# Zero products around two routing stages and a layer boundary of a two-layer trunk, and a new fence for the splits of weights

## The chip, the cores and the metric

The kernel runs on one core of a Trainium2 chip, as one launch. The metric is device time in microseconds; a run's time is that of its slowest core, and here there is only one. Three runs of the kernel before took 848.1, 848.4 and 856.6 us; the median is 848.4 us.

## The reference, cut to what matters

Two layers work on 256 tokens of width 1024. Each layer has two halves:

```
h  = rms_norm(x, g) * (1 + sc1) + sh1          # sc, sh, g come from the condition c
z  = h @ w_in                                  # 1024 x 2840
y  = concat(retention, gmlp, sparse attention) @ w_out
x  = x + g1 * y
h2 = rms_norm(x, g') * (1 + sc2) + sh2
x  = x + g2 * grouped_moe(h2)                  # 16 experts, best group, top 2 in it
```

In `rms_norm` each token is multiplied by `rsqrt(mean(x*x) + eps)`. The router of the mixture needs the logits of all 16 experts, a softmax, the best group of four and the best two experts in it. Only then is it known which tokens go to which expert.

## The kernel before, in words

**Layout.** The residual `xT` lies in SBUF as 128 partitions by 8 chunks by 256 tokens, so a chunk `c` is a block of 128 channels. Everything is float32, and the products that must be exact are made from two float32r parts: an operand is split into a high part `hi` and a low part `lo = x - hi`, and `mm3` makes three products (hi hi, hi lo, lo hi).

**Weights.** They are read from HBM once, in 1 MB pieces, by SyncE's queue into a ring of 11 slots (`slot`, `slots`). A slot is free again when the last product that reads it is done, so the queue runs ahead of TensorE by what the ring holds.

**A layer.** `rms_r` (L312) makes the mean of squares: for each chunk ScalarE squares `xT[:, c, :]` (L316), and TensorE multiplies the square by a constant matrix `onesd` (L317). These eight products, called mean products here, add up in one PSUM bank `pm`. ScalarE then takes a logarithm (L321) and an exponential (L322) of it, which gives `r`. For each chunk VectorE makes `ht` (L420), ScalarE makes the high part `hhi` (L421) and VectorE the low part `hlo` (L422). Then come the input projections `dz` and `tm` (products at L350 to L352, written to `pz`). Each weight block of 128 x 512 is first split by `whl` (L338): ScalarE copies the high part (L344), and VectorE, or GpSimd for one block in three in this layer, subtracts to get the low part (L346). Five buffers hold split blocks. After the mixers come the output projection (`pw`) and the routing stage, called the seam here.

**The seam.** In `moe` VectorE goes through a chain of some thirty small instructions from the logits (`lg`, L873) to the chosen experts (`o1`, L924). TensorE ranks the tokens of each expert with five small products (`prank`, L936 to L940), VectorE makes one-hot tables `Pm` (L1227), TensorE gathers the tokens with them (L980), and the first expert's products (`pgu`, L1051) can begin. The four PSUM banks `mo` that collect the experts' outputs are opened by products of a zero block with zeros (L948), 128 x 512 in bfloat16. `WARM` says how many rounds of four there are: one in the first layer, six in the second.

**The mixture.** Sixteen experts are worked through in four groups: `up` (L1051) or `up_few` (L1060), an activation, a transposition, `down`, and `combine` or `combine_few`, whose products add to `mo`. At the end eight VectorE instructions add `mo` to `xT` (L1310).

**The boundary between the layers.** The mixture of the first layer returns a list `fence`: a product, the last ScalarE instruction that evicts an expert's output, and the last addition to `xT`. In the second layer every split in `whl` is ordered behind the second of these on ScalarE and the third on VectorE, by `tc.issue_after`, which only orders instructions of the same engine.

**What sets the order.** A planner orders each engine's instructions before the kernel runs. It takes them by the order of the program, but an instruction that is not ready by its own estimate of time is passed over for a later one that is. So the zero products at L948 stand after `prank` in the program and run before it. The order is then fixed: each engine works through its instructions in it.

Of the kernel before, what the change touches and what calls it, by code (L numbers as in the profile page):

```python
# [17 lines left out]
S = 256  # L18
# [20 lines left out]
NOVF = 8  # L39
OVE = 12  # L40
OFL = True
WARM = (1, 6)
WV = (0, 1, 5)
NPA = ("0011", "0011")
S4P = ("01111111", "01111111")
# [30 lines left out]
def trunk(tc, I, out):  # L76
    nc = tc.nc
    P = 128
    V, A, G, T, Y = nc.vector, nc.scalar, nc.gpsimd, nc.tensor, nc.sync
# [3 lines left out]
    with ctx:  # L83
# [7 lines left out]
        def tl(cls, shape, name, dt=F32):  # L91
            return up.tile([P] + shape, dt, tag=cls, name=name, bufs=NB[cls])
# [4 lines left out]
        def bank(tag="W", name="pw"):  # L97
            return ps.tile([P, 512], F32, tag=tag if ND else "b", name=name, bufs=(ND if tag == "D" else 8 - ND))
# [24 lines left out]
        onesd = cp.tile([P, P], F32, name="onesd")  # L123
# [15 lines left out]
        def exp_ln_tables():  # L139
            return A.preload_act_table_set("natural_log_exp_and_others")  # L140
# [122 lines left out]
        zb = cp.tile([P, P], BF16, name="zb")  # L263
# [44 lines left out]
        def tables(after):  # L308
            with tc.issue_after(after):
                exp_ln_tables()  # L310

        def rms_r(l, src, last=None):  # L312
            pm = bank("W", "pm")
            for c in range(8):
                sq = tl("k1", [S], "sq")
                sq_ = A.activation(sq, src[:, c, :], AF.Square)  # L316
                T.matmul(pm[:, :S], onesd, sq, start=c == 0, stop=c == 7)  # L317
            if last is not None:
                last(sq_.ins)
            r = tl("k1", [S], "r")  # L320
            A.activation(r, pm[:, :S], AF.Ln, bias=epsc[:, 0:1])  # L321
            A.activation(r, r, AF.Exp, scale=-0.5)  # L322
            return r

        def rms(l, gname, vs, vc, src):
            gs = sml([8], "gs", bufs=2)
            V.scalar_tensor_tensor(gs, mod(l, vc), 1.0, smv(l, gname), op0=OP.add, op1=OP.mult)
            r = rms_r(l, src)
            h = tl("b8", [8, S], "h")
            for c in range(8):  # L330
                t = tl("k1", [S], "ht")
                V.scalar_tensor_tensor(t, src[:, c, :], gs[:, c:c + 1], r, op0=OP.mult, op1=OP.mult)
                A.activation(h[:, c, :], t, AF.Identity, bias=mod(l, vs)[:, c:c + 1])
            return h
# [3 lines left out]
        def whl(wv, n):  # L338
            hl = tl("wh", [2, 512], "whl", F32R)
            hi, lo = hl[:, 0, :n], hl[:, 1, :n]  # L340
            with contextlib.ExitStack() as st:
                for i_ in fence[1:]:
                    st.enter_context(tc.issue_after(i_))
                A.copy(hi, wv)  # L344
                wc[0] += 1
                (G if wc[0] % WP[fl[0]] == 0 else V).tensor_tensor(lo, wv, hi.bitcast(F32), op=OP.subtract)  # L346
            return hi, lo
# [25 lines left out]
        fence = []  # L373
        for l in range(L):
# [30 lines left out]
            if True:  # L405
                pp = up
                r = rms_r(l, xT, angles if l == 0 else tables)
                hhi = tl("b8", [8, S], "hhi", F32R)
                hlo = tl("b8", [8, S], "hlo", F32R)
# [41 lines left out]
                def dz(idx, dst_fn, tag="D"):  # L451
                    pz = [bank(tag, "pz") for _ in range(2)]

                    def step(c):
                        w = whl(ld[f"s{idx}"][c // 4][:, 512 * (c % 4):512 * (c % 4) + 512], 512)
                        for t in range(4):
                            d = slice(P * t, P * t + P)
                            mm3(pz[t // 2][:, S * (t % 2):S * (t % 2) + S], (w[0][:, d], w[1][:, d]),
                                (hhi[:, c, :], hlo[:, c, :]), c == 0 and t % 2 == 0, c == 7)
                        if c == 7:  # L460
                            for t in range(2):
                                dst_fn(2 * t, pz[t].rearrange("p (u n) -> p u n", u=2))
                    return step

                def tm(idx, n, dst_fn, tag="D"):
                    pz = [bank(tag, "pz") for _ in range(2)]

                    def step(c):
                        w = whl(ld[f"s{idx}"][c // 4][:, n * (c % 4):n * (c % 4) + n], n)
                        for tt in range(2):  # L470
                            d = slice(P * tt, P * tt + P)
                            mm3(pz[tt][:, :n], (hhi[:, c, d], hlo[:, c, d]), w, c == 0, c == 7)
                        if c == 7:
                            for tt in range(2):
                                dst_fn(tt, pz[tt])
                    return step
# [42 lines left out]
                for kv in range(2):  # L519
                    pd = bank("W", "pd")  # L520
                    for g in range(2):
                        for hh in range(2):
                            T.matmul(pd[64 * hh:64 * hh + 64, S * g:S * g + S], ident[:, 64 * g:64 * g + 64], zkc[:, kv, :],
                                     start=True, stop=True, skip_group_check=True)
# [237 lines left out]
                for t in range(2):  # L762
                    pg = bank("W", "pg")
                    for n in range(2):
                        for hh in range(2):
                            g = 2 * t + hh
                            T.matmul(pg[64 * hh:64 * hh + 64, P * n:P * n + P], gv[:, n, 64 * g:64 * g + 64], wsT[:, g, :],
                                     start=True, stop=True)
# [7 lines left out]
                def wsplit(k, hf):  # L776
                    return whl(ld[f"o{k // 4}"][k % 4 // 2][:, 1024 * (k % 2) + 512 * hf:1024 * (k % 2) + 512 * hf + 512], 512)
# [20 lines left out]
                for hf in range(2):  # L798
# [21 lines left out]
                    for tt in range(2):  # L820
# [3 lines left out]
                        sq = tl("t2", [512], "sqt")  # L824
# [4 lines left out]
                    for u in range(4):  # L829
                        T.matmul(pq[32 * u:32 * u + 32, :S], rwg[:, 4 * hf + u, :], xT[:, 4 * hf + u, :], start=hf == 0, stop=hf == 1,  # L830
                                 skip_group_check=True)
                lq = tl("k1", [S], "lq")
                V.tensor_copy(lq, pq[:, :S])
                for tt in range(2):
                    T.matmul(pl[:, 16 * tt:16 * tt + 16], lq[:, P * tt:P * tt + P], sel4, start=True, stop=True)
            fence[:] = moe(tc, nc, l, locals())
        for c in (0, 4, 2, 6):
            Y.dma_start(out[:, c:c + 2, :], xT[:, c:c + 2, :])


def moe(tc, nc, l, env):
    g_ = dict(env)
    I, slots, bank, rms, mod, xT = (g_[k] for k in ("I", "slots", "bank", "rms", "mod", "xT"))
    ident, rw, rb, ub, oneb, zb, iot, W4 = (g_[k] for k in ("ident", "rw", "rb", "ub", "oneb", "zb", "iot", "W4"))
    P = 128
    V, A, G, T, Y = nc.vector, nc.scalar, nc.gpsimd, nc.tensor, nc.sync
    reuse = []

    def kept(mk):
        def f(*a, **kw):  # L850
            if not reuse:
                return mk(*a, **kw)
            key = (mk, {"paT": "ppg", "pth": "ppg", "py": "pgx"}.get(a[-1], a[-1])) if mk is bank_ else (mk, a[2] if mk is tl_ else a[1])
            if key not in reuse[0]:
                reuse[0][key] = mk(*a, **kw)
            return reuse[0][key]
        return f
    tl_, sml_, bank_ = g_["tl"], g_["sml"], bank
    tl, sml, bank = kept(tl_), kept(sml_), kept(bank_)
    mp = None  # L860
    if True:
# [84 lines left out]
        mo = [bank("D", f"mo{i}") for i in range(4)]  # L946
        for i in [0, 1, 2, 3] * WARM[l]:
            T.matmul(mo[i], zb, zb.unsqueeze(1).to_broadcast([P, 4, P]), start=True, stop=False, skip_group_check=True)  # L948
# [96 lines left out]
        lastu = [None]  # L1045
# [80 lines left out]
        def combine_few(yy, pT):  # L1126
            for u in range(2):
                for i in range(2):
                    for q in range(4):
                        r_ = slice(SW * q, SW * q + SW)  # L1130
                        T.matmul(mo[q][:, S * u:S * u + S], yy[i][r_, P * u:P * u + P], pT[r_, :], start=False, stop=False,  # L1131
                                 skip_group_check=True)

        def extras():
            cu, capc = g_["cu"], g_["capc"]
# [110 lines left out]
        pm0, last = [None], [None, None, None]  # L1246
        xgs = group(0, lambda tt, p, k: rk[:, tt, ST0 + p:ST0 + p + k])
        pend, seen, done = None, -1, []
        for g4, members in enumerate(XGR):
            order = members  # L1250
            for k, (p, xo_, w) in enumerate(order):
# [23 lines left out]
                def tables_():  # L1275
                    if p == "x":
                        return scatter_tables(one_hot(rkx, w), gP, HOT)
                    if e < NST:
                        return scatter_tables(one_hot(rk[:, :, ST0 + e], w), gate, ST0 + e)
                    return scatter_tables(one_hot(rkP[:, :, e], w), gP, e)  # L1280
# [4 lines left out]
                pT, gc = tables_()  # L1285
                if pend:
                    aT = turn(pend[0])
                    yy = (down_few if pend[4] else down)(aT, *pend[1:4])
# [15 lines left out]
                if seen == RES:  # L1304
                    last[2] = lastu[0]
        done.pop(0)()
        combine_few(down_few(turn(pend[0]), *pend[1:4]), pend[2])
        for m in (0, 2, 4, 6, 1, 3, 5, 7):
            b, u = m // 2, m % 2
            last[1] = V.scalar_tensor_tensor(xT[:, m, :], mo[b][:, S * u:S * u + S], mod(l, 5)[:, m:m + 1], xT[:, m, :],  # L1310
                                   op0=OP.mult, op1=OP.add).ins
        return [last[2]] + last[:2]


def pack(inp):
# [73 lines left out]
```

## Time and profile before

| what | value |
|---|---|
| runs | 848.1, 848.4, 856.6 us, median 848.4 |
| the profiled execution | 856.05 us |
| its span, first to last instruction | 854.5 us |
| TensorE busy | 762.8 us (89%) |
| VectorE busy | 459.3 us (54%) |
| ScalarE busy | 273.4 us (32%) |
| mean granted clock of TensorE | 0.929 of full speed |
| read from HBM | 290.84 MB |

Read the table with the span in mind: 1.55 us of the profiled execution lie around it. TensorE is granted full speed (1.00, the 2.4 GHz level) or half of it (0.50, the 1.2 GHz level); a mean between them in a stretch says that the clock changed in it. A busy TensorE at half speed is doing half the work. The profiled execution is one of the longer ones: it stands 7.65 us above the median of the runs.

### The profile page before, as it was taken

What the parts mean: (1) busy time and instruction counts of PE and PEld (TensorE: products, weight loads), DVE (VectorE), ACT (ScalarE), POOL (GpSimd) and SP (SyncE); (2) the same over time, 40 slices, a digit from 0 to 9 for tenths busy, and PEclk for the clock granted to TensorE, in tenths of its full rate; (3) what the DMA queues carried; (4) which work ended last, traced back from release to release, by engine and by line L of the source; (5) the groups of instructions that cost most, each with busy time, mean ns of one, the idle gap of its engine ahead of it and who ended that gap; (6) DMA issues with size and microseconds to landing.
All of it is one profiled execution on the core that took longest, in us unless ns stands there. A gap on an engine that the chain in (4) does not pass through costs nothing. (4 is left out here: it accounts for less than half of the span.)

```text
span 854.5 us, 14344 instructions
## 1 busy us (share of the span) xinstructions
PE 762.8 (89%) x5460; PEld 480.2 (56%) x5460; DVE 459.3 (54%) x1189; ACT 273.4 (32%) x655; POOL 68.0 (8%) x83
## 2 busy tenths in 40 slices
PE   3789999976999999887988998999999999979795
PEld 2677665775535455343448886678744545534342
DVE  6997959986833223211245998598582322312123
ACT  6246555633111111110135646466311201101010
POOL 2232200120000000000003231002000000000000
PEclk9899869979899999989999996699999999998798
DMA  8959818979799999999999489178878999999993
GB/s 354 420 224 354 321 45 296 395 275 383 304 381 418 417 418 419 418 420 413 421 417 379 156 300 389 58 265 323 318 283 303 359 421 415 419 418 418 416 418 145
DMA packets 47169, 292.95 MB, mean 343 GB/s; under 512 B 5488, under 2 KB 6256, under 8 KB 16496
## 3 DMA queue, kind: packets, MB, share of 16 engines
q1 hardware_dynamic: 45648, 289.76, 85.3%
q10 hardware_dynamic: 1440, 2.16, 0.8%
q8 instruction: 46, 0.75, 0.3%
q14 instruction: 35, 0.29, 0.1%
HBM read 290.84 MB, written 1.05 MB: 342 GB/s over the span
## 5 line engine op out<-in xcount | busy, mean ns | idle before, releaser
L1051 PE MATMUL pgu<-w1slot,xg 128*64 128x512 f32 x640 | 168.5, 623 | 18.3 <-PEq L1188 9.8
L1051 PEld LDWEIGHTS pgu<-w1slot,xg 128*64 128x64 f32 x640 | 51.7, 141 | 101.0 <-issue 97.9
L193 DVE SCALAR_TENSOR_TENSOR adaslot<-adaslot,sb__90 128x1024 f32<-128x1024 f32 x72 | 94.5, 1324 | 0.0
L1093 DVE SCALAR_TENSOR_TENSOR yy<-py,gc,yy 64x512 fp32r<-64x512 f32 x40 | 30.0, 750 | 108.6 <-ACT yy L1092 108.6
L350 PE MATMUL pz<-hhi,whl 128*128 128x256 f32 x256 | 75.0, 304 | 10.2 <-ACT hhi L421 10.2
L351 PE MATMUL pz<-hlo,whl 128*128 128x256 f32 x256 | 76.1, 301 | 0.9 <-DVE hlo L422 0.7
L352 PE MATMUL pz<-hhi,whl 128*128 128x256 f32 x256 | 76.3, 304 | 0.5 <-DVE whl L346 0.4
L1092 ACT ACTIVATE yy<-py,gc 64x512 fp32r<-64x512 f32 x40 | 27.3, 683 | 151.5 <-PE py L1084 135.3
L346 POOL TENSOR_TENSOR whl<-winslot,whl 128x512 fp32r<-128x512 f32 (+1 forms) x24 | 34.2, 1425 | 370.7 <-DMA winslot<-win_dram 239.7
L1060 PE MATMUL pgu<-w1slot,xg 128*32 128x256 f32 x896 | 58.4, 382 | 5.2 <-DMA w1slot<-w_dram 5.2
L350 PEld LDWEIGHTS pz<-hhi,whl 128*128 128x128 f32 x256 | 51.1, 205 | 14.4 <-ACT hhi L421 13.1
L351 PEld LDWEIGHTS pz<-hlo,whl 128*128 128x128 f32 x256 | 52.5, 205 | 3.0 <-DVE hlo L422 1.7
L352 PEld LDWEIGHTS pz<-hhi,whl 128*128 128x128 f32 x256 | 51.9, 204 | 3.6 <-issue 2.1
L1040 DVE CAST pgT<-ppg 128x256 fp32r<-128x256 f32 x34 | 14.4, 424 | 72.3 <-PE ppg L1038 72.3
L344 ACT CAST whl<-winslot 128x512 fp32r<-128x512 f32 (+1 forms) x72 | 40.7, 576 | 26.6 <-PE pz L352 25.4
L1067 DVE TENSOR_TENSOR a<-a,pgu 128x256 f32<-128x256 f32 (+1 forms) x34 | 12.4, 365 | 65.6 <-ACT a L1066 65.4
L1060 PEld LDWEIGHTS pgu<-w1slot,xg 128*32 128x32 f32 x896 | 28.6, 109 | 33.8 <-issue 16.5
L1066 ACT ACTIVATE a<-pgu 128x256 f32<-128x256 f32 (+1 forms) x34 | 11.6, 340 | 108.4 <-PE pgu L1051 91.7
L350 PE MATMUL pw<-yhi,whl 128*128 128x256 f32 x128 | 37.6, 295 | 5.5 <-DVE mod L194 3.9
L1101 ACT ACTIVATE yy<-py,gc 128x256 fp32r<-128x256 f32 x14 | 6.6, 473 | 108.6 <-PE py L1109 108.6
L346 DVE TENSOR_TENSOR whl<-winslot,whl 128x512 fp32r<-128x512 f32 (+1 forms) x48 | 33.7, 707 | 10.0 <-ACT whl L344 9.9
L352 PE MATMUL pw<-yhi,whl 128*128 128x256 f32 x128 | 36.9, 295 | 2.3 <-DVE whl L346 2.2
(506 smaller groups left out, 1455.7 us busy)
## 6 DMA issues: line engine op xcount, KB each, us to landing
w1slot<-w_dram SPq DMA_DIRECT2D x128, 1024.0 KB, 16.2
adaslot<-adaw_dram SPq DMA_DIRECT2D x40, 1024.0 KB, 7.0
wd<-wd_dram SPq DMA_DIRECT2D x30, 1024.0 KB, 14.7
winslot<-win_dram SPq DMA_DIRECT2D x14, 1024.0 KB, 16.1
slot<-adaw_dram SPq DMA_DIRECT2D x8, 1024.0 KB, 18.5
woslot<-wout_dram SPq DMA_DIRECT2D x8, 1024.0 KB, 11.6
slot<-win_dram SPq DMA_DIRECT2D x6, 1024.0 KB, 17.5
cmpslot<-cmpw_dram SPq DMA_DIRECT2D x4, 1024.0 KB, 13.5
```

What stands on the lines that cost most here:

```text
L193: V.scalar_tensor_tensor(wb, wb, 1.0, sb_, op0=OP.mult, op1=OP.mult, accum_out=mv_[:, b:b + 1])
L344: A.copy(hi, wv)
L346: (G if wc[0] % WP[fl[0]] == 0 else V).tensor_tensor(lo, wv, hi.bitcast(F32), op=OP.subtract)
L350: T.matmul(o, a[0], b[0], start=start, stop=False, skip_group_check=True)
L351: T.matmul(o, a[0], b[1], start=False, stop=False, skip_group_check=True)
L352: T.matmul(o, a[1], b[0], start=False, stop=stop, skip_group_check=True)
L1040: V.tensor_copy(pT, pp_[:, :S])
L1051: lastu[0] = T.matmul(gu[64 * j:64 * j + 64, :], xg(c)[:, xs:xs + CAP], w1(c, j), start=c == 0, stop=c == 7, skip_group_check=True).ins
L1060: lastu[0] = T.matmul(gu[SW * t:SW * t + SW, 0:256], xg(c)[:, xs:xs + SW], wv, start=c == 0, stop=c == 7, skip_group_check=True).ins
L1067: V.tensor_tensor(a, a, gu[:, n:2 * n], op=OP.mult)
L1092: ya = A.activation(y[0:64, :], py[r_, :], AF.Copy, scale=gc[r_, :])
L1093: V.scalar_tensor_tensor(y[64:128, :], py[r_, :], gc[r_, :], y[0:64, :].bitcast(F32), op0=OP.mult, op1=OP.subtract)
```

## The change

It does three things.

1. `WARM` goes from (1, 6) to (6, 8). The first layer's seam gets 24 zero products in place of 4, and the second layer's 32 in place of 24.
2. A new helper `spin` issues zero products into a bank of their own, which nobody reads. At the boundary three of them are ordered behind the last product of the mixture's last `combine_few`, ahead of the mean products, and eight behind the last mean product. This is done where `fence` is not empty, so in the second layer alone.
3. In the second layer ScalarE's copies in `whl` are ordered behind the last square of `rms_r` and no longer behind the last eviction of an expert. VectorE's subtractions are still ordered behind the last addition to `xT`, GpSimd's behind nothing but their data.

```diff
-WARM = (1, 6)
+WARM = (6, 8)
...
+        def spin(n, after):
+            wz = bank("W", "wz")
+            with tc.issue_after(after):
+                for _ in range(n):
+                    T.matmul(wz, zb, zb.unsqueeze(1).to_broadcast([P, 4, P]), start=True, stop=True, skip_group_check=True)
+
         def rms_r(l, src, last=None):
+            if fence:
+                spin(3, fence[3])
             pm = bank("W", "pm")
             for c in range(8):
                 sq = tl("k1", [S], "sq")
                 sq_ = A.activation(sq, src[:, c, :], AF.Square)
-                T.matmul(pm[:, :S], onesd, sq, start=c == 0, stop=c == 7)
+                pm_ = T.matmul(pm[:, :S], onesd, sq, start=c == 0, stop=c == 7)
             if last is not None:
                 last(sq_.ins)
+            if fence:
+                fence[1] = sq_.ins
+                spin(8, pm_.ins)
...
-                for i_ in fence[1:]:
+                for i_ in fence[1:3]:
                     st.enter_context(tc.issue_after(i_))
                 A.copy(hi, wv)
...
-                        T.matmul(mo[q][:, S * u:S * u + S], yy[i][r_, P * u:P * u + P], pT[r_, :], start=False, stop=False,
-                                 skip_group_check=True)
+                        lastu[0] = T.matmul(mo[q][:, S * u:S * u + S], yy[i][r_, P * u:P * u + P], pT[r_, :], start=False,
+                                            stop=False, skip_group_check=True).ins
...
-        return [last[2]] + last[:2]
+        return [last[2]] + last[:2] + [lastu[0]]
```

## Rows read from the trace of the kernel before

**Rows 1.** The cores view: span and mean granted clock of TensorE.

```profile
core 0: 854.5 us, clock 0.929
```

**Rows 2.** Stretches at the seams: start:end, length, busy us (instructions) by engine, clock, DMA share, GB/s.

```profile
209.00:213.84 4.84, 0.53 (x2) 0.10 (x1) 3.35 (x25) 3.52 (x10) 0.00 (x0) 0.98 1.00 416
213.84:220.48 6.64, 5.57 (x30) 5.51 (x30) 4.60 (x19) 0.56 (x1) 0.00 (x0) 0.50 0.97 398
220.48:224.10 3.62, 3.62 (x24) 2.09 (x23) 3.12 (x6) 2.79 (x4) 0.00 (x0) 1.00 0.02 9
224.10:438.00 213.90, 196.79 (x1507) 96.22 (x1506) 62.48 (x199) 28.51 (x55) 0.00 (x0) 0.98 1.01 410
...
613.58:618.71 5.13, 4.69 (x24) 2.04 (x24) 3.46 (x28) 3.68 (x11) 0.00 (x0) 1.00 1.00 367
...
619.99:623.98 3.99, 3.99 (x32) 3.86 (x33) 3.96 (x9) 1.33 (x3) 0.00 (x0) 1.00 0.20 80
```

**Rows 3.** TensorE's waits within 224 to 440 us: waited for, total us, times, longest.

```profile
PE pgu L1051 <- DMA w1slot<-w_dram: 4.5, 2, 3.9
```

**Rows 4.** Timeline of TensorE, first seam: start, length, what [idle before <- releaser].

```profile
213.90 0.17 PE L936 MATMUL prank<-o,ub 128*128 128x16 bf16 x1 [3.64 <-DVE o L924]
...
215.19 3.75 PE L980 MATMUL pgx<-Pm,hi 128*128 128x256 f32 x16 [1.01 <-DVE Pm L1227]
...
221.52 1.94 PE L1051 MATMUL pgu<-w1slot,xg 128*64 128x512 f32 x8
```

**Rows 5.** Timeline of TensorE, second seam.

```profile
613.58 4.69 PE L948 MATMUL mo<-zb 128*128 128x512 bf16 x21
618.71 0.17 PE L936 MATMUL prank<-o,ub 128*128 128x16 bf16 x1 [0.44 <-DVE o L924]
...
619.99 2.15 PE L980 MATMUL pgx<-Pm,hi 128*128 128x256 f32 x16 [1.01 <-DVE Pm L1227]
...
623.98 1.94 PE L1051 MATMUL pgu<-w1slot,xg 128*64 128x512 f32 x8
```

**Rows 6.** Stretches at the boundary, after it, and two long ones at the low clock.

```profile
445.90:449.90 4.00, 4.00 (x12) 3.03 (x11) 1.74 (x3) 2.95 (x6) 0.89 (x1) 0.59 1.00 414
...
452.20:456.00 3.80, 3.64 (x16) 3.44 (x17) 3.80 (x11) 2.66 (x6) 0.00 (x0) 0.55 1.01 416
456.00:517.00 61.00, 60.25 (x456) 51.49 (x455) 54.02 (x91) 31.75 (x62) 18.30 (x12) 1.00 0.74 271
520.90:548.90 28.00, 28.00 (x99) 19.09 (x99) 15.79 (x52) 15.51 (x61) 2.05 (x2) 0.51 0.42 174
101.00:121.50 20.50, 20.50 (x64) 12.09 (x63) 12.35 (x40) 10.52 (x42) 1.27 (x1) 0.50 0.40 166
```

**Rows 7.** Timeline of TensorE at the boundary.

```profile
445.16 4.97 PE L317 MATMUL pm<-sq,onesd 128*128 128x256 f32 x14 [0.73 <-ACT sq L316]
452.21 0.50 PE L350 MATMUL pz<-hhi,whl 128*128 128x256 f32 x2 [2.07 <-ACT hhi L421]
```

**Rows 8.** Timeline of VectorE at the boundary.

```profile
442.60 3.23 DVE L1310 SCALAR_TENSOR_TENSOR xT<-mo,mod,xT 128x256 f32<-128x256 f32 x8 [0.53 <-PE mo L1131]
445.75 1.89 DVE L346 TENSOR_TENSOR whl<-winslot,whl 128x512 fp32r<-128x512 f32 x3
```

**Rows 9.** Timeline of ScalarE at the boundary.

```profile
442.22 1.14 ACT L344 CAST whl<-winslot 128x512 fp32r<-128x512 f32 x2 [0.85 <-DMA winslot<-win_dram]
...
443.58 1.12 ACT L344 CAST whl<-winslot 128x512 fp32r<-128x512 f32 x2
444.69 2.26 ACT L316 ACTIVATE sq<-xT 128x256 f32<-128x256 f32 x7
446.96 1.28 ACT L140 ACT_TABLE_LOAD   x1
448.26 0.62 ACT L344 CAST whl<-winslot 128x512 fp32r<-128x512 f32 x1
450.18 0.47 ACT L321 ACTIVATE r<-pm,epsc 128x256 f32<-128x256 f32 x1 [1.30 <-PE pm L317]
```

## The prediction

> **What bounds the kernel now.** I began with the cores view: 854.5 us at a mean clock of 0.929 [rows 1]. A mean of 0.929 between the levels 1.00 and 0.50 means 2 x 0.071 x 854.5 = 121 us at the low one. So the first question for every stage is at which level it runs, and the second whether TensorE or the weight stream ends last there.
>
> The stretches answer both. In the first mixture the DMA share is 1.01 over 213.9 us, and TensorE at times waits for a weight slot [rows 2, 3]: the stream from HBM sets the pace. But it stops at the seam: in the 3.62 us ahead of 224.1 its share is 0.02, because all slots are full until TensorE consumes them [rows 2]. So a microsecond by which TensorE starts the experts earlier restarts the stream a microsecond earlier, and the mixture ends that much earlier. In the second layer's front TensorE is busy 60.25 of 61.00 us with a DMA share of 0.74 [rows 6]: there it is the bound itself, and what it gains at the boundary travels through the second seam to the end.
>
> The clock falls in all three places. In the first seam TensorE has 0.53 us of work in 4.84 us, and the next 6.64 us are at 0.50 [rows 2]. At the boundary the mean products run at a mean of 0.59 for 4.00 us, and after an idle 2.07 us the first projection runs at 0.55 for 3.80 us [rows 6, 7]. The second seam, filled with zero products, stays at 1.00 [rows 2, 5].
>
> **First seam: 20 more zero products.** The second layer has just this form today: 24 products, 21 of them in 4.69 us, 0.223 us each, then `prank` after 0.44 us idle [rows 5]. In the first layer `prank` waits 3.64 us for the same `o` [rows 4], so twenty more products fill it and a little before it, as in layer two, and delay nothing if the planner places them alike. The price of the low clock is read from the two seams: first gather to first expert product takes 221.52 - 215.19 = 6.33 us in the first and 623.98 - 619.99 = 3.99 us in the second [rows 4, 5]. Gain 2.34 us. It is smaller than the 3.62 us for which the stream stands still [rows 2], so the stream takes it whole. Ends: 0 to 2.34; a loss I exclude, since the same number of products in the same chain made `prank` late by nothing in layer two.
>
> **Second seam: 8 more.** Clock 1.00 already, so no gain. They are 8 x 0.223 = 1.78 us of work. The idle time still there is 0.44 us before `prank` and 1.01 us before the gather [rows 5], 1.45 us. The products stand behind `prank` in the program, so those the planner can't fit before it go behind it. What doesn't fit is 0.33 us, my value; if all eight run ahead of `prank` the cost is 1.78 - 0.44 = 1.34 us, and if they find room later, 0.
>
> **Boundary, three products ahead of the means.** 3 x 0.223 = 0.67 us in TensorE's idle time before the second chunk's square; no cost. If they hold the clock, the stretch 445.9 to 449.9 is at full speed: its 4.00 us of products take 2.0, and the means end at 450.13 - 2.0 = 448.1 in place of 445.16 + 4.97 = 450.13 [rows 6, 7]. ScalarE's table load ends at 446.96 + 1.28 = 448.24, so the logarithm could issue there in place of 450.18, 1.94 us earlier [rows 9]. I take off one split copy of 0.62 us, because today the planner puts one between the table load and the logarithm [rows 9]: gain 1.3 us.
>
> **Eight products behind the means.** 1.78 us at full speed, and TensorE has 2.07 us idle there [rows 7]: covered. If the clock stays up, the 3.80 us of projection at 0.55 [rows 6] take about half: gain 1.9 us. If it doesn't, the eight cost up to 3.57 us and overrun the idle time by 1.5.
>
> **The fence.** Four copies run today before the last seven squares, in two pairs of 1.14 and 1.12 us [rows 9]. One would think that they hold the squares up. They don't: the second chunk's addition is the fifth of eight that take 3.23 us from 442.60, so it ends near 442.60 + 5/8 x 3.23 = 444.62, and the square starts at 444.69 [rows 8, 9]. The fence gains 0.1 us at most. What it costs: the copies leave idle time and queue behind the table load, with the logarithm, the exponential and `hhi`, and the three subtractions of 1.89 us that VectorE did while it had nothing else [rows 8] now compete with `ht` and `hlo`, on which the projection waits. I take 1.9 us, these three, since VectorE feeds the projection. Ends: 0, and 2.88 + 1.89 = 4.77 us for all five copies (1.14 + 1.12 + 0.62) and the three in line.
>
> **Sum.** Boundary: -1.3 - 1.9 + 1.9 = -1.3 us. Whole: -2.34 - 1.3 + 0.33 = -3.3 us, against the profiled execution's own 856.05 us: 852.7. That execution is 7.65 us above the median of 848.4, with the same instructions; I carry the difference over: 848.4 - 3.3 = 845.1 us. The ends are -2.34 - 1.94 - 1.9 = -6.2 us, and +4.77 + 1.34 = +6.1 with no gain of clock at all.
>
> **The skill beside it.** By rows the three falls of the clock are worth 2.34 + 1.94 + 1.9 = 6.2 us, 0.7% of the span, and the whole trace has 121 us at the low level [rows 1]. The Trainium skill, "TensorE: Matmul & The Clock Gate", Part 1, "What's actually happening", says that the penalty of the ramp is under 1% of a typical span and shouldn't be fitted to a count of slow products. By that rule alone the clock's terms would be left out and the sum would be +2.2 us; the rows price the first seam by two runs of one code, so the sum keeps them. For the whole trace the rows disagree: 121 us at half speed are 14% of the span.
>
> **Rivals.**
>
> *The fence decides (slower).* Place: ScalarE between the table load's end at 448.24 and the first `hhi`. If the planner puts all five copies before the logarithm, that one issues at 448.24 + 2.88 = 451.12, 0.94 us later than today, the three subtractions add 1.89, and the longer wait lets the clock fall again, so nothing is gained there: +2.83 us, with the seams -2.34 + 0.33: +0.8, so 849.2 us. It decides once the first projection product issues over 2.0 us later behind the last addition than today's 452.21 - 445.83 = 6.38 us. For it: ScalarE is in order. Against: the logarithm stands ahead of the copies in the program, and one copy alone went first. Chance 0.12.
>
> *The falls are not the kernel's (no gain).* Executions of one code lie 8.5 us apart, 848.1 to 856.6, so some stretch at half speed is there in one and not in another. If those of the seam and the boundary are missing in the median run, or the products don't hold the clock, only the added work is left: 0.33 and some of the fence's 1.9, about 849.5 us. The Trainium skill, same page and section, says that the gate watches free of the kernel's start, so where a change falls varies from run to run; this trace is one execution and cannot show it. Against: the idle seam is so empty, 0.53 us of work in 4.84, that I'd expect the fall in most executions. Chance 0.2.
>
> *A long stretch at half speed appears or goes.* TensorE works at half speed for 20.5 us from 101 and for 28.0 us from 520.9 [rows 6], while the weight stream is slack. The second comes behind the boundary, and a start moved by some microseconds and another order can spare it or lengthen it. By the spread of the runs that is about 8 us: 837 or 853. Chance 0.07 and 0.09.
>
> **How the numbers follow.** Forecast as worked out, 840 to 848: chance 0.52. The likeliest single case gives 845.1. Range 839.5 to 853.5: it holds the forecast, the fence, no gain and the longer stretch, and its lower end lies just under the sum's best end, 842.2, with some of the spread. By 1%, 8.5 us, which is about what a measurement of this kernel can tell from no change, the borders are 839.9 and 856.9. Below lie the shorter stretch and a tail of the forecast: 0.10. Above lie the longer stretch together with the fence's dear end: 0.06. The rest is 0.84.
>
> **What would show it.** Right: clock 1.00 in the first seam and about 4.0 us from first gather to first expert product; at the boundary 1.00 through means and projection, the logarithm within 1 us of the table load's end, and the first projection product some 5 us behind the last addition. Wrong: zero products still running when `o` is done in the second seam, by up to 1.3 us; copies in a row before the logarithm; TensorE waiting for `whl` on VectorE in the first projection; or the clock low at the boundary in spite of the products. The forecast falls whole if the mixture's stream doesn't restart earlier although the first expert does.

## The result, and the profile after

The changed kernel takes **853.35 us** in the median of 20 runs (846.92 to 862.41), the kernel before 847.76 us in 20 (843.97 to 862.78). The ratio is 1.006 with a 95% interval of 1.0035 to 1.0085: **slower by 0.6%**, some 5 us. Forecast were 845.1 us and a gain of 3.3. The time lies in the range, at its upper edge, and the sign was wrong.

The profiled execution took 854.99 us. Its cores view:

```profile
core 0: 853.4 us, clock 0.943
```

The span is 1.1 us *shorter* than that of before, at a higher clock [rows 1]. So these two executions, laid side by side, hide the loss; why is shown below. First the stretches, with the columns of [rows 2]:

```profile
214.96:220.24 5.28, 4.27 (x38) 4.07 (x37) 5.24 (x19) 1.33 (x3) 0.00 (x0) 1.00 0.90 373
220.24:224.00 3.76, 3.76 (x21) 1.66 (x22) 3.46 (x8) 1.95 (x3) 0.00 (x0) 1.00 0.24 50
...
445.20:448.60 3.40, 3.36 (x16) 2.79 (x17) 0.71 (x2) 3.37 (x8) 0.00 (x0) 1.00 1.02 424
...
458.70:465.20 6.50, 6.10 (x28) 6.10 (x29) 2.85 (x5) 1.23 (x2) 1.28 (x1) 0.50 0.76 234
...
526.00:537.00 11.00, 11.00 (x40) 6.48 (x41) 9.23 (x25) 6.23 (x26) 1.42 (x1) 0.53 1.02 428
```

The seam and the mean products are at full speed now; they were at 0.50 and 0.59 [rows 2, 6]. But the first projection has a fall of its own, 6.5 us at 0.50 from 458.7. The last line is why the two profiles mislead: the long half-speed stretch behind the boundary, 28.0 us in the profile of before [rows 6], is some 11 us here. The timeline of TensorE in the first seam:

```profile
212.20 2.32 PE L959 MATMUL mo<-zb 128*128 128x512 bf16 x10
214.96 0.17 PE L947 MATMUL prank<-o,ub 128*128 128x16 bf16 x1 [0.44 <-DVE o L935]
...
216.24 2.15 PE L991 MATMUL pgx<-Pm,hi 128*128 128x256 f32 x16 [1.01 <-DVE Pm L1238]
...
220.24 1.94 PE L1062 MATMUL pgu<-w1slot,xg 128*64 128x512 f32 x8
```

From the first gather to the first expert product it is 4.00 us, as against 6.33 [rows 4]. The same engine in the second seam:

```profile
613.52 5.56 PE L959 MATMUL mo<-zb 128*128 128x512 bf16 x25
618.91 0.17 PE L947 MATMUL prank<-o,ub 128*128 128x16 bf16 x1
...
619.04 1.02 PE L959 MATMUL mo<-zb 128*128 128x512 bf16 x4
620.08 2.14 PE L991 MATMUL pgx<-Pm,hi 128*128 128x256 f32 x16
...
624.06 1.94 PE L1062 MATMUL pgu<-w1slot,xg 128*64 128x512 f32 x8
```

No idle time stands ahead of `prank` and of the gather any more, where it was 0.44 and 1.01 us [rows 5]: the products fill both places. TensorE at the boundary:

```profile
442.59 0.82 PE L316 MATMUL wz<-zb 128*128 128x512 bf16 x3
...
445.24 3.29 PE L325 MATMUL pm<-sq,onesd 128*128 128x256 f32 x14 [0.87 <-ACT sq L324]
448.36 1.89 PE L316 MATMUL wz<-zb 128*128 128x512 bf16 x8
452.06 0.50 PE L361 MATMUL pz<-hhi,whl 128*128 128x256 f32 x2 [1.81 <-ACT hhi L432]
...
456.05 0.28 PE L362 MATMUL pz<-hlo,whl 128*128 128x256 f32 x1
459.10 0.58 PE L363 MATMUL pz<-hhi,whl 128*128 128x256 f32 x1 [2.78 <-DVE whl L357]
```

The three products run ahead of the first mean product, in idle time, and the mean products take 3.29 us in place of 4.97 [rows 7]. The last line is new: the projection is under way and stops for 2.78 us, for a low half (`whl`, L357) from VectorE. After this stop the clock is at 0.50. What VectorE did meanwhile:

```profile
442.69 3.23 DVE L1321 SCALAR_TENSOR_TENSOR xT<-mo,mod,xT 128x256 f32<-128x256 f32 x8 [0.52 <-PE mo L1142]
448.99 0.69 DVE L357 TENSOR_TENSOR whl<-winslot,whl 128x512 fp32r<-128x512 f32 x1 [3.08 <-ACT whl L355]
450.19 2.47 DVE L431 SCALAR_TENSOR_TENSOR ht<-xT,gs,r 128x256 f32<-128x256 f32 x4 [0.51 <-ACT r L333]
452.58 1.66 DVE L433 SCALAR_TENSOR_TENSOR hlo<-ht,mod,hhi 128x256 fp32r<-128x256 f32 x4
454.16 2.70 DVE L431 SCALAR_TENSOR_TENSOR ht<-xT,gs,r 128x256 f32<-128x256 f32 x4
456.78 1.66 DVE L433 SCALAR_TENSOR_TENSOR hlo<-ht,mod,hhi 128x256 fp32r<-128x256 f32 x4
458.37 2.49 DVE L357 TENSOR_TENSOR whl<-winslot,whl 128x512 fp32r<-128x512 f32 x4
```

Before, three low halves followed the additions at once [rows 8]. Now VectorE idles for 3.08 us there, because the copies don't exist yet, makes one, and then takes up all eight `ht` and all eight `hlo`. The next four low halves start at 458.37, 8.18 us after the first `ht`; TensorE resumes when the first of them is there. The eight `ht` (shortest, median and longest in ns) and GpSimd's subtractions at the same time:

```profile
L431 DVE SCALAR_TENSOR_TENSOR ht<-xT,gs,r x8: 472/473/1509, 450.2 to 456.4; 128x256 f32<-128x256 f32 x8
449.92 1.27 POOL L357 TENSOR_TENSOR whl<-winslot,whl 128x512 fp32r<-128x512 f32 x1 [240.87 <-ACT whl L355]
453.85 1.54 POOL L357 TENSOR_TENSOR whl<-winslot,whl 128x512 fp32r<-128x512 f32 x1 [2.66 <-ACT whl L355]
```

The first `ht` (450.19 to 451.47) and the fifth (454.16 to 455.67) each ran beside one of them, took 1.28 and 1.51 us, and ended 0.28 us behind it; the others took about 0.47. Before, no subtraction of GpSimd ran beside the eight `ht`, and all took 0.48. So about 1.8 of the 8.18 us are these two; no run tried them apart. ScalarE:

```profile
444.77 2.26 ACT L324 ACTIVATE sq<-xT 128x256 f32<-128x256 f32 x7 [1.15 <-DVE xT L1321]
447.04 1.28 ACT L140 ACT_TABLE_LOAD   x1
448.34 0.62 ACT L355 CAST whl<-winslot 128x512 fp32r<-128x512 f32 x1
448.86 0.47 ACT L332 ACTIVATE r<-pm,epsc 128x256 f32<-128x256 f32 x1
449.23 0.61 ACT L355 CAST whl<-winslot 128x512 fp32r<-128x512 f32 x1
449.74 0.41 ACT L333 ACTIVATE r<-r 128x256 f32<-128x256 f32 x1
450.06 1.12 ACT L355 CAST whl<-winslot 128x512 fp32r<-128x512 f32 x2
451.50 1.70 ACT L432 ACTIVATE hhi<-ht,mod 128x256 fp32r<-128x256 f32 x4 [0.32 <-DVE ht L431]
```

One copy stands before the logarithm, as before, one between it and the exponential, two before the first `hhi`. That one is released by the slow first `ht` (0.32 us), not by the copies, which end at 451.18. Last, TensorE's waits from 443 to 700 us, in the columns of [rows 3]:

```profile
PE pz L363 <- DVE whl L357: 3.7, 3, 2.8
PE pz L362 <- DVE whl L357: 1.8, 1, 1.8
```

### The profile page after: what moved, and what is told of

The parts are those of the page before. It is cut to its first block, busy times and chain, and to the rows that moved or that the text cites. A ratio compares the mean times of both kernels' runs of the same rounds, so it can differ in the third digit from the quotient of the medians.

```text
span 853.4 us, 14426 instructions
## 1 busy us (share of the span) xinstructions
PE 761.3 (89%) x5499; PEld 475.8 (56%) x5499; DVE 461.6 (54%) x1189; ACT 272.8 (32%) x655; POOL 67.8 (8%) x83
## 4 chain that ended last, share of the span: by engine, by line
PE 26%; DMA 13%; DVE 10%; issue 2%; ACT 2%; SPq 0%; DVEq 0%; ACTq 0%
DMA w1slot<-w_dram 8%; PE pgu L1062 7%; PE py L1095 3%; DVE adaslot L193 3%; DMA wd<-wd_dram 2%; DVE whl L357 2%; PE pgu L1071 2%; DMA wd__8077<-wd_dram 2%; DMA wd__8221<-wd_dram 2%; PE py L1120 1%; PE mo L1134 1%; PE pgx L991 1%; PE pz L363 1%; PE mo L959 1%; PE pz L362 1%
## 5 line engine op out<-in xcount | busy, mean ns | idle before, releaser
L193 DVE SCALAR_TENSOR_TENSOR adaslot<-adaslot,sb__90 128x1024 f32<-128x1024 f32 x72 | 91.4, 1281 | 0.0
L361 PE MATMUL pz<-hhi,whl 128*128 128x256 f32 x256 | 73.7, 299 | 12.0 <-ACT hhi L432 12.0
L363 PE MATMUL pz<-hhi,whl 128*128 128x256 f32 x256 | 75.6, 301 | 3.9 <-DVE whl L357 3.7
L357 POOL TENSOR_TENSOR whl<-winslot,whl 128x512 fp32r<-128x512 f32 (+1 forms) x24 | 34.4, 1433 | 368.3 <-ACT whl L355 327.1
L357 DVE TENSOR_TENSOR whl<-winslot,whl 128x512 fp32r<-128x512 f32 (+1 forms) x48 | 35.8, 754 | 16.5 <-ACT whl L355 16.4
```

Source lines behind the costliest of these rows:

```text
L193: V.scalar_tensor_tensor(wb, wb, 1.0, sb_, op0=OP.mult, op1=OP.mult, accum_out=mv_[:, b:b + 1])
L361: T.matmul(o, a[0], b[0], start=start, stop=False, skip_group_check=True)
L363: T.matmul(o, a[1], b[0], start=False, stop=stop, skip_group_check=True)
```

## The experiments

Each kernel is the changed one with the edit shown, so line numbers are those of the profile after; each was timed in five rounds against the kernel before. To compare executions that began at different times, I count from **the end of the last addition to `xT`** (442.69 + 3.23 = 445.92 us in the profile after). The stations are the logarithm's start, the first product `pz`, the end of the first projection's first half (the copy `zkc`) and the first product of the compressed attention (`pk`).

| kernel | log. | pz | zkc | pk |
|---|---|---|---|---|
| before | 4.35 | 6.38 | 18.81 | 75.00 |
| after, the whole change | 2.94 | 6.14 | 23.39 | 83.56 |
| e1_warm | 5.46 | 7.50 | 20.05 | 76.83 |
| e2_fence | 4.12 | 7.32 | 21.71 | 81.46 |
| e3_spin | 2.95 | 5.31 | 16.26 | 72.41 |
| e4_warm_spin | 2.99 | 5.36 | 16.29 | 72.52 |
| e5_interleave | 2.95 | 6.15 | 19.32 | 78.07 |
| e7_no_three | 4.34 | 6.37 | 17.31 | 73.24 |
| e8_no_eight | 2.95 | 5.32 | 17.93 | 73.98 |
| e9_warm66 | 2.95 | 5.32 | 16.25 | 72.45 |

Each row is one execution. e1_warm has the boundary of the kernel before and is 1.1 us later at the logarithm and 1.8 us at `pk`; its mean products took 6.10 us. e3_spin, e4_warm_spin and e9_warm66, whose clock holds at the boundary, agree within 0.11 us at every station. `pk` is also not the same amount of work in all rows: 384 products `pz` run ahead of it in after and e2_fence, 379 in e5_interleave, 372 in the others.

**The parts alone.** My theory was that the fence costs more than everything else gains; the rival, that the products don't pay and the loss comes from the clock's falls elsewhere.

Seams alone (e1_warm):

```diff
-                spin(3, fence[3])
+                pass
...
-                fence[1] = sq_.ins
-                spin(8, pm_.ins)
+                pass
```

> The change with only its first part: WARM = (6, 8), no products at the boundary, the old fence. Theory (the fence is what costs: it puts VectorE's low halves behind ht and hlo): no loss here; first gather to first expert product 4.0 us in both seams, prank in the second seam late by at most 0.3 us, time 0 to 2.3 us below the kernel before, 845.5 to 848. Rival (the zero products of the seams cost): about 853, as with the whole change. Rival (the clock falls in the mixture whatever the seam does, and gives the 2.3 us back): the time of the kernel before, 847.8.

Measured: 844.65 us (13 runs), ratio 0.9969 (0.9941 to 0.9997), a little below the theory's 845.5 to 848. In its profile the first seam takes 5.26 us from `prank` to the first expert product, 7.62 before. The seams gain a little; the interval just clears 1.

Fence alone (e2_fence):

```diff
-WARM = (6, 8)
+WARM = (1, 6)
...
-                spin(3, fence[3])
+                pass
...
-                spin(8, pm_.ins)
+                pass
```

> The kernel before with only the new fence: ScalarE's splits in the second layer behind the last square, no added products anywhere. Theory (the fence costs): slower by 4 to 8 us, 852 to 856; TensorE waits over 2 us for a low half on VectorE in the first projection of the second layer, and the clock falls behind that wait. Rival (the added products cost): the time of the kernel before, 847.8, within 1.5 us.

Measured: 853.7 us (11 runs), ratio 1.0085 (1.0052 to 1.0119). TensorE's timeline:

```profile
445.67 4.75 PE L325 MATMUL pm<-sq,onesd 128*128 128x256 f32 x14 [0.87 <-ACT sq L324]
453.66 0.50 PE L361 MATMUL pz<-hhi,whl 128*128 128x256 f32 x2 [3.24 <-ACT hhi L432]
```

The means are slow as before, the projection starts 0.94 us later than before and then waits for low halves; at `pk` it is 6.5 us behind. The time is as the theory said, the place only in part: the longest wait for a low half in the first projection is 1.1 us, not over 2, and the half speed (0.51 from 455.4 to 458.8) stands ahead of it. Alone the fence makes the kernel slower by about as much as the whole change does (the two intervals overlap), so the loss is its.

Products at the boundary alone (e3_spin):

```diff
-WARM = (6, 8)
+WARM = (1, 6)
...
-                fence[1] = sq_.ins
+                pass
```

> The kernel before with only the eleven zero products at the boundary, WARM = (1, 6) and the old fence. Theory (the fence costs, the products help): granted clock 1.00 from the means through the first projection; the means end near 448, the first projection product issues about 5 us behind the last addition to xT in place of 6.4, and the first 96 products of the projection end some 3 us earlier: 844 to 846. Rival (the products at the boundary cost): 851 to 854, with the first projection product late by up to 1.8 us.

Measured: 847.2 us (12 runs), ratio 0.9977 (0.9944 to 1.0011): above the theory's 844 to 846 and not told apart from no change. The trace is clear where the time isn't: `zkc` 2.55 us earlier, `pk` 2.59.

All without the fence (e4_warm_spin):

```diff
-                fence[1] = sq_.ins
+                pass
```

> The whole change without its fence: WARM = (6, 8) and the eleven products at the boundary, splits ordered as before. Theory (the fence costs): the best of the four, 842 to 846, 7 to 11 us below the whole change. Rival (the added products cost): 852 to 854, as the whole change. If it lies at 847 to 849 the clock's gains are given back somewhere later, and the trace has to show where.

Measured: **841.92 us** (838.14 to 846.01, 12 runs), ratio 0.994 (0.9913 to 0.9967). It beats both kernels: its interval lies wholly below 1, that of the whole change wholly above. One line is worth 853.35 - 841.92 = 11.4 us by the medians, 1.006 / 0.994 = 1.2% or 10.3 us by the ratios. TensorE at its boundary:

```profile
442.83 3.29 PE L325 MATMUL pm<-sq,onesd 128*128 128x256 f32 x14 [0.65 <-ACT sq L324]
445.96 1.89 PE L316 MATMUL wz<-zb 128*128 128x512 bf16 x8
448.83 0.50 PE L361 MATMUL pz<-hhi,whl 128*128 128x256 f32 x2 [0.98 <-ACT hhi L432]
```

VectorE and ScalarE there:

```profile
443.39 1.88 DVE L357 TENSOR_TENSOR whl<-winslot,whl 128x512 fp32r<-128x512 f32 x3
447.41 1.62 DVE L431 SCALAR_TENSOR_TENSOR ht<-xT,gs,r 128x256 f32<-128x256 f32 x3 [2.13 <-ACT r L333]
448.95 1.26 DVE L433 SCALAR_TENSOR_TENSOR hlo<-ht,mod,hhi 128x256 fp32r<-128x256 f32 x3
```

```profile
441.34 1.12 ACT L355 CAST whl<-winslot 128x512 fp32r<-128x512 f32 x2
442.37 2.25 ACT L324 ACTIVATE sq<-xT 128x256 f32<-128x256 f32 x7
```

And two stretches of it, the projection and the place of the long half-speed stretch:

```profile
448.60:458.00 9.40, 9.03 (x77) 8.82 (x78) 8.89 (x19) 6.26 (x14) 2.02 (x1) 1.00 1.00 410
...
520.00:550.00 30.00, 29.47 (x179) 19.64 (x177) 26.70 (x80) 21.60 (x80) 1.87 (x1) 0.95 0.58 217
```

Without the fence the low halves fill VectorE's idle time, `ht` and `hlo` come in threes, and the projection runs at 1.00 throughout. The copies end with the addition that the squares wait for and hold nothing up.

**Whether the order on VectorE is the fence's whole price** (e5_interleave). The whole change, fence included, but each chunk's `ht`, `hhi` and `hlo` stand in the program just ahead of the projection step that uses them:

```diff
-                    for c in range(8):
+                    for c in range(0):
...
-                    run(dz(0, s0), lambda c: fill(FILL[l][8][c]))
+                    run(lambda c: hchunk(c) if c >= 0 else None, dz(0, s0), lambda c: fill(FILL[l][8][c]))
```

> The whole change, fence included, but in the second layer each chunk's ht, hhi and hlo stand in the program just ahead of that chunk's weight split, so that VectorE makes the third chunk's low half ahead of the first hlo and not behind the eighth. Theory (the fence costs because the low halves queue behind ht and hlo on VectorE): the 2.8 us wait of TensorE for a low half and the fall of the clock behind it go, and most of the fence's 11 us comes back: 842 to 846. Rival (what costs is ScalarE, where the copies stand between the squares and hhi): the first projection product is late as before, no wait less, 851 to 855.

Measured: 849.14 us (12 runs), ratio 1.0021 (0.9991 to 1.0052). TensorE's timeline:

```profile
449.80 0.50 PE L361 MATMUL pz<-hhi,whl 128*128 128x256 f32 x2 [1.81 <-ACT hhi L432]
451.05 0.39 PE L362 MATMUL pz<-hlo,whl 128*128 128x256 f32 x1 [0.75 <-DVE hlo L433]
```

The time lies between the theory and the rival. The stop for a low half in the first projection is gone, and of the 23.39 - 16.29 = 7.1 us that the fence costs at `zkc`, 4.07 come back. The other 3 do not: `hhi` is still late (1.81 us idle, 0.98 without the fence), a low half now pushes `hlo` back (0.75 us), and the clock is at 0.57 from 452 to 455.8. At `zkc` VectorE's order is thus the larger part, not the whole. By time only a third comes back (0.4 of 1.2%), and this run's interval reaches to 1.0052, that of the whole change down to 1.0035: how the price divides over the whole kernel is not settled.

**Which products hold which work.** e4_warm_spin without the three (e7_no_three) and without the eight (e8_no_eight):

```diff
-                spin(3, fence[3])
+                pass
```

> The whole change without its fence and without the three zero products ahead of the means; the eight behind them stay. Theory (the three hold the clock through the means): the clock falls again during the means, the logarithm issues some 2 us later behind the last addition, while the first projection still runs at 1.00: 843 to 845, 1.5 to 2.5 us above the kernel with both. Rival (the eight alone do it): 842 and the means at 1.00.

```diff
-                spin(8, pm_.ins)
+                pass
```

> The whole change without its fence and without the eight zero products behind the means; the three ahead of them stay. Theory (the eight hold the clock for the first projection): means at 1.00, then some 2.5 us idle, and the first projection begins at half speed for about 3.8 us: 843 to 845. Rival (with the means fast the clock doesn't fall again): 842 and the projection at 1.00.

Measured: 846.39 us, ratio 0.9971 (0.9928 to 1.0014), and 846.51 us, 0.9982 (0.9939 to 1.0024). Both medians lie above the theories' 843 to 845, but by time neither is told apart from e4_warm_spin. The traces tell them apart; TensorE without the three:

```profile
443.12 4.98 PE L325 MATMUL pm<-sq,onesd 128*128 128x256 f32 x14 [0.77 <-ACT sq L324]
...
450.17 0.50 PE L361 MATMUL pz<-hhi,whl 128*128 128x256 f32 x2 [0.35 <-ACT hhi L432]
```

and without the eight:

```profile
440.33 3.29 PE L325 MATMUL pm<-sq,onesd 128*128 128x256 f32 x14 [0.80 <-ACT sq L324]
446.33 0.69 PE L361 MATMUL pz<-hhi,whl 128*128 128x256 f32 x2 [2.70 <-ACT hhi L432]
```

Without the three the means take 4.98 us again; without the eight, 2.70 us idle stand ahead of the projection, and the clock is at 0.52 from 446.3 to 449.8. At `zkc` the three are worth 17.31 - 16.29 = 1.0 us and the eight 17.93 - 16.29 = 1.6, each in one execution.

**The second seam's eight** (e9_warm66), e4_warm_spin with

```diff
-WARM = (6, 8)
+WARM = (6, 6)
```

> The whole change without its fence, with WARM = (6, 6) in place of (6, 8). The rows of the changed kernel show prank 0.26 us later behind the zero products with 32 than with 24, and the gather 0.15 us later: 842, not to be told from the kernel with 32. Rival (32 hold the clock of the second seam in runs in which 24 don't): 843 to 845, with a wider spread.

Measured: 845.24 us (838.17 to 852.9), ratio 0.9952 (0.9913 to 0.9992). Median and spread are about as the rival said, but the interval overlaps that of e4_warm_spin: inconclusive by time. In its profile the second seam stays at 1.00 with 24 products, so nothing of the rival's mechanism shows. By trace `prank` to the first expert product is 5.28 us with 24 products and 5.15 with 32.

## Why the prediction was wrong

**First seam, -2.34: right.** The seam is at 1.00, and from `prank` to the first expert product it shortens by 7.62 - 5.28 = 2.34 us. The first expert product comes at 220.24 in place of 221.52, though `prank` came 1.06 us later in this execution, and the stream is back sooner: SyncE's next weight transfer issues 7.26 us behind `prank` (222.22) in place of 9.60 (223.50). In these two profiles little of it is left at the mixture's end, 442.69 and 442.60 for the start of the last additions, because behind a stop of 4.84 us TensorE ran at a mean of 0.57 from 396 to 408 us; the low clock there lasted from 398 to 402 in the profile before. That fall does not go with the change: it lasts for 10.2 us in e2_fence and e3_spin, which have the first seam of before, and for 3.4 us in e5_interleave and e7_no_three, which have the new one. Over all ten profiles the gain reaches the end: from `prank` to the start of the last additions it is 226.4 to 227.7 us in the seven with 24 products and 228.7 to 229.8 in the three with 4.

**Second seam, +0.33: about right.** `prank` starts 0.31 us behind the end of `o`, 0.06 before, and the gather 1.17 us behind `prank` in place of 1.28: 0.15 us later in all.

**The means, -1.3: right.** 2.94 against 4.35 is 1.41 us, and one copy stands before the logarithm as assumed. One step in it was misread and did no harm: 4.00 us at a mean of 0.59 hold 4.00 x 0.59 = 2.4 us of work at full speed, not 2.0, so 1.6 us were to be won in the means; they became 4.97 - 3.29 = 1.68 us shorter, and the copy hid the difference.

**The projection's clock, -1.9: about right, but only without the fence.** By the same reading 3.80 us at 0.55 give 1.7 us, and the eight gave 1.6. With the fence the fall came back behind a new wait.

**The fence: the step that failed.** "I take 1.9 us, these three, since VectorE feeds the projection." That is the duration of the three displaced subtractions, on VectorE alone. The runs show 1.2%, over twice even the upper end of 4.77 us. It goes, at `zkc`, into 7.1 us: VectorE idles for 3.08 us where the low halves stood, and what is displaced doesn't come back at its own length but behind the sixteen `ht` and `hlo`, 8.18 us of work; TensorE stops for 2.78 us and then runs 6.5 us at half speed. The 83.56 - 72.52 = 11.0 us at `pk` overstate what follows, since 12 products `pz` and two `pin` more run ahead of it with the fence. At the 372nd product `pz`, the same count in both, it is 77.83 - 69.10 = 8.7 us, 1.6 more than at `zkc`. That is idle time: from `zkc` to there TensorE is busy for 51.88 of 54.44 us, 51.92 of 52.81 in e4_warm_spin. In this stretch the planner's order of ScalarE and VectorE is another one in the three fenced kernels; without the fence, e3_spin and e4_warm_spin keep the order of before. Which of those swaps costs how much was not tried, and what of the 10.3 us lies behind the 8.7 is open; by the two intervals together the 1.2% are some 7 to 13 us (an estimate). So the mechanism had been named among the signs ("TensorE waiting for `whl` on VectorE in the first projection"), and its size taken from the wrong row: the length of the work instead of the queue in front of it.

Without the fence's term the forecast is -3.3 - 1.9 = -5.2 us. e4_warm_spin, which is the change without it, measured 0.6%, -5.1 us (-7.4 to -2.8 by its interval). The other terms stand; that the two agree to 0.1 us is luck, as the interval says. e9_warm66, with a forecast of -5.5, measured -4.1.

**The skill's rule beside it.** The Trainium skill, "TensorE: Matmul & The Clock Gate", Part 1, "What's actually happening", puts the ramp's penalty under 1% of a typical span, and by that rule the clock's terms would have been left out. What the zero products win here is 0.6%, so its size fits this part; left out of the sum it would have cost the whole gain. For all the low clock of the trace it doesn't fit: the mean of 0.943 means 2 x 0.057 x 853.4 = 97 us at half speed, 11% of the span, of which full speed would save at most half, 49 us or 6% (an estimate). The prediction set the whole 121 us, 14%, beside the rule, where at most half of it is a penalty.

**The rivals.** *The fence decides* had the sign, and the place wrong. By its own point it did not decide: the first `pz` issues 6.14 us behind the last addition, earlier than before, and at it the fence costs 0.78 us (6.14 against 5.36): about 0.3 by the copy between logarithm and exponential, the rest by the first `ht`, which takes 1.28 us in place of 0.82. The price fell behind that point. *The falls are not the kernel's* is out: the first seam is at 1.00 in all seven profiles with 24 products and at half speed in all three with 4, and the mean products are at 1.00 in all six with the three products ahead of them and fall in all four without. *The long stretch* does not explain the loss. Over all runs the median of the mean clock is 0.942 after and 0.934 before (34 runs), that is 99 us at half speed and 112: the changed kernel is slower although its clock is higher. What it lost is time in which TensorE waits or is slow at the boundary and shortly behind it, not that stretch. The stretch does account for the two profiles' near equal spans: from `pk` to the router's logits (`pl`) they take 71.8 us after and 80.5 before, and the 8.6 us by which it is behind at `pk` are gone by then.

## What to carry to other kernels

Here an ordering edge that held back filler work cost what the queue in which that work landed made of it, not the work's length: ask what stands ahead of it when it is released, and which engine starves meanwhile. Zero products in idle time are worth pricing stage by stage against a sibling stage that runs at full speed; here that gave 5.2 us forecast, without the fence's term, and 5.1 (2.8 to 7.4) measured. And when a change has several parts, time the whole without each: the fastest kernel here is the change less one line.

## What the runs showed of the hardware

- The clock after a gap: 2.78 us idle in the projection and 2.70 us ahead of it (e8_no_eight) were followed by half speed for 6.5 and some 3.5 us; 0.98 us (e4_warm_spin) was not. The zero products behind the means left 1.81 us in the changed kernel, and the first 4 us of its projection were at 1.00; in e5_interleave 1.81 us and 0.75 us close behind it were followed by 0.57 from 452 to 455.8.
- Half speed can stay on a busy TensorE. In the 30 us from 520 e4_warm_spin has it busy for 29.47 us at a mean of 0.95; e3_spin, with the same order of products up to `pk`, for 30.00 us at 0.67. In all seven profiles without the fence this half speed begins beside a wait of 3.1 us for `hid` ahead of `pk`, from 0.3 us ahead of the wait's end to 1.6 us behind it; in the kernel before at 520.9:

```profile
520.83 0.38 PE L551 MATMUL pk<-hid,sm 128*64 128x15 f32 x4 [3.12 <-DVE hid L137]
```

  How long it lasts differs: 27.3 us there, 3.4 us in e7_no_three. No run took the wait away alone, so that it starts the stretch is likely and not shown, and what ends it is open. Over all executions the kernel before ran at mean clocks from 0.923 (859.38 us) to 0.950 (843.35 us).
- VectorE beside GpSimd: two `ht` that ran beside a subtraction of GpSimd took 1.28 and 1.51 us and ended 0.28 us behind it; the other six took about 0.47 us.
